# A two-layer decoder trunk: a new beginning, the exponential's table loaded ahead of the attention, and the compression's inner chain in five VectorE operations

## Chip, cores and metric

The kernel runs on 1 core of one Trainium2 chip. The time is the device time of one execution in microseconds (us); less is better.

## What is computed

A trunk of two layers over 256 tokens of width 1024, in float32. Each layer norms x, multiplies it by one wide matrix, and cuts the result into the inputs of two attentions and two merge gates:

```python
def hybrid_layer(x, ...):
    h = rms_norm(x, attn_pre_gain)
    u = h @ w_in
    (qa, ka, va, qb, kcb, vcb, ksb, vsb, kwb, vwb, g_nsa, g_a, g_b) = jnp.split(u, offsets, axis=-1)
    o_a = swa_sink_attention(rope(qa), rope(ka), va, attn_sinks)
    kc = compress(kcb, cmp_pos_emb[0], cmp_w1[0], cmp_b1[0], cmp_w2[0])
    vc = compress(vcb, cmp_pos_emb[1], cmp_w1[1], cmp_b1[1], cmp_w2[1])
    o_b = nsa_attention(qb, rope(qb), kc, vc, rope(ksb), vsb, rope(kwb), vwb, sigmoid(g_nsa))
    mixed = jax.nn.sigmoid(g_a) * (o_a @ w_branch_a) + jax.nn.sigmoid(g_b) * (o_b @ w_branch_b)
    x = x + rms_norm(mixed @ w_out, attn_post_gain)
    x = x + rms_norm(conv_ffn(rms_norm(x, ffn_pre_gain), ...), ffn_post_gain)

def compress(t, pos_emb, w1, b1, w2):
    # blocks of 32 tokens at a stride of 16, flattened
    hid = jax.nn.gelu((blocks + pos_emb) @ w1 + b1, approximate=True)
    return hid @ w2
```

The calls that are cut or shortened here (`...`, `rope`) are as their names say. The compression turns the 256 tokens into 15 blocks for keys and again for values, in each layer: four chains of it in all.

## The kernel before, in words

**Products in three parts.** Every float32 operand is split into a rounded high part and the remainder, the low part, and each product is three TensorE matmuls: high by high (L366), high by low weight (L367), low x by high weight (L368). The 256 tokens are two row blocks of 128, called t = 0 and 1.

**Weights.** The stream `W` holds all weights in the order of use. A chunk is loaded (`load`) by a DMA issued on SyncE's queue (SP) into one of four buffers `st`; ScalarE copies it to the rounded `wh` (L114, through `copy`), VectorE subtracts to get `wl` (L117, through `sub`). These two lines are helpers: the same lines stand for every such split in the kernel. `make` does both, `high` does ScalarE's part and hands back VectorE's.

**Input projection.** `w_in` is cut into nine tiles of up to 512 columns (`IN_TILES`); a tile has four chunks c of two 128-row steps, and for each chunk the two row blocks t, so 4 x 2 x 2 x 3 = 48 matmuls. What follows a tile is its `fin_...`: for the first, queries of the first attention, a rotation (`rope`, L466 to L470), the split of the result (`q_rot`) and, some ticks later, transposes on TensorE (L477) whose result ScalarE copies to SBUF. The third tile to be computed holds the columns from 1536 on.

**Order.** A clock counts the parts of work that the program writes out; `later(n, fn)` puts `fn` n ticks behind. For most of the program the framework's scheduler then orders instructions by its own rules; in the first tile the written order is kept on TensorE, VectorE and ScalarE (`MANUAL0`). The first tile takes its parts (t, c) in the order `FIRST`, and `HOOKS` says what comes ahead of which part: the steps 1, 2, 3 (make that weight chunk), B, C, D (transpose and split another quarter of X) and r (`rest`: norms of the rows, the rope tables).

**Beginning** (`start`, from L1117). TensorE runs 6 matmuls of zeros (`warm`, L1124), a transpose of the gain, four transposes of X's first quarter (`first_T`, L410; one quarter is 128 rows by 512 columns), then 8 more matmuls of zeros, and then the first tile. X comes in three transfers: the first quarter on ScalarE's queue, the second on SP behind W0, the other half of X on SP behind W1. Then W2, W3 and the small inputs follow on SP. `table(fn)` (L270, L271) runs a one-element activation so that ScalarE loads that function's table: Sin at the start, for the rope tables.

**First attention.** `Unit.scores` runs score matmuls (L595), a row minimum on VectorE for each head (L604) and an exponential on ScalarE (L607). The first exponential makes ScalarE load that table, since the sine's is in place.

**Compression** (`cmp_hidden_T`, from L724). Two transposes, a VectorE copy out of PSUM (L733), then nine operations of GpSimd (POOL, L736 to L747): three add up a bias, three add shifted parts of the hidden values to it, and three build the cubic in the tanh of the gelu. Some ticks later `cmp_gelu` runs the tanh on ScalarE (L753) and VectorE goes on from there (L754).

## Time and profile before

| | us |
|---|---|
| three runs | 791.46, 794.11, 797.75 |
| their median | 794.11 |
| the profiled execution, its own time | 794.85 |
| its span in the profile | 793.0 |

The span is the time from the first to the last instruction in the trace; the execution's own time is 1.85 us longer, for what lies around it. In the profile the engines are PE (TensorE), PEld (its weight load), DVE (VectorE), ACT (ScalarE), POOL (GpSimd) and SP (SyncE). PEclk is the clock granted to TensorE as a share of full speed. A wait is shown as [idle before <-what ended it]. A row such as "x3" at its end is a group of three instructions of the same kind, and its duration is theirs together.

### The profile page before, as it was taken

The numbers are of one execution on the slowest core, as the hardware profiler recorded it, in microseconds if no ns is written. First come the engines' busy times: TensorE is split into PE (matmuls) and PEld (weight loads), VectorE is DVE, ScalarE is ACT, GpSimd is POOL, SyncE is SP. The second block draws the span as 40 slices with busy tenths as digits, with TensorE's granted clock in tenths as the row PEclk, the third lists the DMA queues.
The fourth block names the chain that finished last, engine by engine and source line by source line (L and its number), as shares of the span: only waits on it lengthen the run. The fifth ranks groups of instructions, "written<-read, shape, count | busy, mean of one in ns | idle before, by whom it ended". The sixth has DMA issues, their size and how long they took to land.

```text
span 793.0 us, 12908 instructions
## 1 busy us (share of the span) xinstructions
PE 765.7 (97%) x4745; PEld 682.0 (86%) x4745; DVE 613.2 (77%) x1168; ACT 495.4 (62%) x948; POOL 48.1 (6%) x96
## 2 busy tenths in 40 slices
PE   8999999999899999999989999999998999999996
PEld 6689888888699999999868889888877999999995
DVE  5898888676778767777788888886867877778775
ACT  4678877744666555665555879767555655556552
POOL 2300022100100000000010000230001000000000
PEclk9999999999999999999999999999999999999999
DMA  7633156456556656666435232644645666656731
GB/s 268 218 111 123 41 160 216 144 172 205 166 168 196 187 185 183 209 218 186 157 118 173 74 121 86 206 151 135 205 137 182 193 185 186 186 184 212 216 105 53
DMA packets 42202, 131.26 MB, mean 166 GB/s; under 512 B 5359, under 2 KB 5915, under 8 KB 42139
## 3 DMA queue, kind: packets, MB, share of 16 engines
q1 hardware_dynamic: 41995, 130.18, 51.4%
q8 instruction: 37, 0.61, 0.3%
q10 hardware_dynamic: 144, 0.26, 0.1%
q14 instruction: 26, 0.21, 0.1%
HBM read 129.37 MB, written 1.05 MB: 164 GB/s over the span
## 4 chain that ended last, share of the span: by engine, by line
PE 81%; DVE 7%; ACT 7%; POOL 2%; issue 2%; DMA 1%; SPq 0%; DVEq 0%; POOLq 0%; ACTq 0%
PE mm L366 6%; PE mm L367 6%; PE mm L368 6%; PE S L367 5%; PE S L368 5%; PE S L366 5%; PE T L1000 5%; PE T L999 5%; PE mm L1000 5%; PE mm L999 5%; PE T L998 5%; PE mm L998 5%; PE O L366 3%; PE O L367 3%; PE O L368 3%; DVE wl L117 2%
## 5 line engine op out<-in xcount | busy, mean ns | idle before, releaser
L117 DVE TENSOR_TENSOR wl<-st,wh 128x1024 fp32r<-128x1024 f32 (+2 forms) x226 | 268.0, 1188 | 101.1 <-ACT wh L114 99.7
L114 ACT ACTIVATE wh<-st 128x1024 fp32r<-128x1024 f32 (+2 forms) x226 | 231.8, 1029 | 170.9 <-PE O L368 40.1
L366 PE MATMUL mm<-wh,x 128*128 128x512 f32 (+2 forms) x256 | 97.3, 382 | 0.1
L367 PE MATMUL mm<-wl,x 128*128 128x512 f32 (+2 forms) x256 | 96.2, 376 | 0.0
L368 PE MATMUL mm<-wh,x 128*128 128x512 f32 (+2 forms) x256 | 95.2, 372 | 0.0
L999 PE MATMUL mm<-q,wh 128*128 128x256 f32 x320 | 90.7, 283 | 0.0
L999 PE MATMUL T<-q,wh 128*128 128x256 f32 x320 | 90.6, 283 | 0.0
L1000 PE MATMUL T<-q,wl 128*128 128x256 f32 x320 | 90.6, 283 | 0.0
L1000 PE MATMUL mm<-q,wl 128*128 128x256 f32 x320 | 90.5, 283 | 0.0
L998 PE MATMUL T<-q,wh 128*128 128x256 f32 x320 | 90.5, 283 | 0.0
L998 PE MATMUL mm<-q,wh 128*128 128x256 f32 x320 | 90.4, 283 | 0.0
L998 PEld LDWEIGHTS mm<-q,wh 128*128 128x128 f32 x320 | 61.3, 192 | 0.9
L998 PEld LDWEIGHTS T<-q,wh 128*128 128x128 f32 x320 | 61.4, 192 | 0.8
L999 PEld LDWEIGHTS mm<-q,wh 128*128 128x128 f32 x320 | 61.3, 192 | 0.8
L999 PEld LDWEIGHTS T<-q,wh 128*128 128x128 f32 x320 | 61.4, 192 | 0.7
L1000 PEld LDWEIGHTS mm<-q,wl 128*128 128x128 f32 x320 | 61.3, 192 | 0.1
L1000 PEld LDWEIGHTS T<-q,wl 128*128 128x128 f32 x320 | 61.4, 192 | 0.0
L368 PEld LDWEIGHTS mm<-wh,x 128*128 128x128 f32 x256 | 49.2, 192 | 6.3
L366 PEld LDWEIGHTS mm<-wh,x 128*128 128x128 f32 x256 | 49.2, 193 | 5.8 <-ACT k L114 0.4
L367 PEld LDWEIGHTS mm<-wl,x 128*128 128x128 f32 x256 | 49.4, 193 | 5.6 <-DVE wl L117 0.3
L607 ACT ACTIVATE k<-k,mn 128x128 f32<-128x128 f32 (+1 forms) x96 | 42.5, 446 | 8.4 <-DVE mn L604 8.4
L354 POOL TENSOR_SCALAR rstd<-s 128x1 f32<-128x1 f32 x16 | 6.1, 381 | 520.7 <-ACT k L362 520.5
(293 smaller groups left out, 1672.9 us busy)
## 6 DMA issues: line engine op xcount, KB each, us to landing
st<-in_ffn_w_up_dram SPq DMA_DIRECT2D x88, 512.0 KB, 4.3
st<-in_w_in_dram SPq DMA_DIRECT2D x48, 512.0 KB, 3.8
st<-in_ffn_w_down_dram SPq DMA_DIRECT2D x44, 512.0 KB, 4.3
st<-in_w_out_dram SPq DMA_DIRECT2D x16, 512.0 KB, 3.6
st<-in_w_in_dram SPq DMA_DIRECT2D x16, 384.0 KB, 3.1
st<-in_cmp_w_dram SPq DMA_DIRECT2D x16, 256.0 KB, 2.6
st<-in_w_branch_a_dram SPq DMA_DIRECT2D x8, 512.0 KB, 3.6
st<-in_w_branch_b_dram SPq DMA_DIRECT2D x8, 512.0 KB, 3.6
```

The costliest lines, as they stand in the source:

```text
L114: act.activation(dst, src, AF.Copy, scale=scale)
L117: dve.tensor_tensor(dst, a, b, ALU.subtract)
L354: pool.tensor_scalar(r, s2[:, 0:1], s2[:, 1:2], EPS, ALU.add, ALU.add)
L366: pe.matmul(o, xh, wh, start=first, stop=False, skip_group_check=True)
L367: pe.matmul(o, xh, wl, start=False, stop=False, skip_group_check=True)
L368: pe.matmul(o, xl, wh, start=False, stop=last, skip_group_check=True)
L607: last_exp[0] = act.activation(self.pt[:, hh, s, :], sm[:, :nk], AF.Exp, bias=self.mn[:, i:i + 1], scale=-1.0, accum_out=self.dn[:, i:i + 1])
L998: pe.matmul(o, wh[:, k, :], hh[:, k, c0:c1], start=(k == 0), stop=False, skip_group_check=True)
L999: pe.matmul(o, wh[:, k, :], hl[:, k, c0:c1], start=False, stop=False, skip_group_check=True)
L1000: pe.matmul(o, wl[:, k, :], hh[:, k, c0:c1], start=False, stop=(k == 7), skip_group_check=True)
```

## The change

It has three parts. **First, the beginning.** All four quarters of X are issued on ScalarE's queue, the two first halves ahead of the two second halves, and W0 to W3 alone stand first on SP. Chunks 4 to 9 are loaded early, right behind the small constants, into buffers that later hold other things (tags "sg" and "kB"), not into the four `st`. `WARM` becomes 6, 2 and 3 matmuls, with X's transposes between them. The first two chunks of the first tile are no longer done part by part but by `products`: for chunk 0, both row blocks are taken in the order high by high, high by low weight, low x by high weight; for chunk 1 each row block has high by high, low x by high weight, high by low weight. The second halves of X are transposed in one step (`second`) ahead of the third part, W3 is made ahead of the fifth, and `rest` ahead of the sixth.

**Second, the table of the exponential.** `table(AF.Exp)` is run behind the rope tables in layer 1, and behind the first copy of the first tile's rotation for t = 1 in layer 2. **Third, the compression.** The nine POOL operations become five on VectorE, each with two arithmetic steps; the bias b1 is added in the third of them.

```diff
...
-WARM = (6, 8)
-HOOKS = {0: '1C', 1: 'B2', 2: 'D', 6: '3r'}
-FIRST = [(0, 0), (0, 1), (1, 0), (1, 1), (0, 2), (1, 2), (0, 3), (1, 3)]
+WARM = (6, 2, 3)
+FIRST = [(0, 0), (1, 0), (0, 1), (1, 1), (0, 2), (1, 2), (0, 3), (1, 3)]
+EARLY = {4: ("sg", 2), 6: ("sg", 2), 8: ("kB", 1)}
 CMPI = (0, 0, 0, 0, 4, 6, 7, 8)
...
     def copy(dst, src, scale=1.0):
-        act.activation(dst, src, AF.Copy, scale=scale)
+        return act.activation(dst, src, AF.Copy, scale=scale)
...
     class Stream:
         def __init__(self):
             self.specs, self.loaded, self.made, self.used, self.front = [], {}, {}, 0, 0
+            self.room = {}
         def add(self, src, a, b, tag="w", ahead=2):
             self.specs.append((src, a, b, tag, ahead))
...
         def load(self, i):
             src, a, b, tag, _ = self.specs[i]
-            st = wp.tile([P, a, b], F32, tag="st", bufs=4, name=nm("st"))
+            st = self.room.pop(i, None)
+            if st is None:
+                st = wp.tile([P, a, b], F32, tag="st", bufs=4, name=nm("st"))
             nc.sync.dma_start(st, src)
             self.loaded[i] = st, a, b, tag
+        def early(self, i, tag, bufs):
+            both = ap_.tile([P, 2, 2, 512], F32, tag=tag, bufs=bufs, name=nm("early"))
+            self.room[i], self.room[i + 1] = both[:, 0], both[:, 1]
         def make(self, i=None):
             i = self.front if i is None else i
...
     pool.memset(rows, 0.0)
     grow = k1()[0:KD, 0:P]
     nc.sync.dma_start(cst[:, 0:P], consts[:, 0:P])
-    act.dma_start(halves(X[:, 0, :])[0], halves(xv[:, 0, :])[0])
     nc.sync.dma_start(grow, attn_pre_gain[0].rearrange("(k p) -> k p", p=P))
-    W.load(0)
-    nc.sync.dma_start(halves(X[:, 0, :])[1], halves(xv[:, 0, :])[1])
-    W.load(1)
-    nc.sync.dma_start(X[:, 1, :], xv[:, 1, :])
-    W.load(2)
-    W.load(3)
+    for h in range(2):
+        for t in range(2):
+            act.dma_start(halves(X[:, t, :])[h], halves(xv[:, t, :])[h])
+    for i in range(4):
+        W.load(i)
     last_sq = [None]
     def table(fn):
...
     nc.sync.dma_start(cst[:, P:], consts[:, P:])
     sink = cp.tile([P, DEPTH, 8], F32, name="sink")
     nc.sync.dma_start(sink, attn_sinks.partition_broadcast(P))
+    for i, (tag, bufs) in EARLY.items():
+        W.early(i, tag, bufs)
+        W.load(i)
+        W.load(i + 1)
     row_load(R_B1, cmp_b1.rearrange("l k h -> (l k) h"))
     row_load(R_POS, cmp_pos_emb.rearrange("l k (pr two) d -> (l k pr) (two d)", two=2))
...
         SG = [ap_.tile([P, QKV], F32, tag="sg", bufs=2, name=nm("SG")) for _ in range(2)]
         done = set()
+        def products(t, c, bk, chs, w):
+            todo = [(tt, p, k) for p in ((0, 0), (0, 1), (1, 0)) for tt in range(2) for k in range(2)] if c == 0 else \
+                   [(t, p, k) for p in ((0, 0), (1, 0), (0, 1)) for k in range(2)]
+            if c == 0:
+                todo = todo[6 * t:6 * t + 6]
+            for tt, (xp_, wp_), k in todo:
+                tk = slice(tt * P, (tt + 1) * P)
+                pe.matmul(bk[tt][:, :w], (xh, xl)[xp_][:, 2 * c + k, tk], chs[c][wp_][:, k, :],
+                          start=(c == k == xp_ == wp_ == 0), stop=False, skip_group_check=True)
         def in_tile(i, tag, fin, tmajor=False, hooks={}):
             c0, w = IN_TILES[i]
             bk = [bank(tag) for _ in range(2)]
...
                     chs[c] = W.next(2, w)
                 ch = chs[c]
                 tk = slice(t * P, (t + 1) * P)
+                if first and i == 0 and c < 2:
+                    products(t, c, bk, chs, w)
+                    return
                 for k in range(2):
                     kk = 2 * c + k
                     o, wh, wl = bk[t][:, :w], ch[0][:, k, :], ch[1][:, k, :]
...
                 done.add(key)
             return fn
-        def q_rot(qT, t, h0, src, key, delays):
+        def q_rot(qT, t, h0, src, key, delays, exp_after=None):
             d = rope(src, t, True, 4 * len(delays))
             for i, delay in enumerate(delays):
                 stk = k2(F32R)
                 sv = stk.rearrange("p (h a d) -> p h a d", h=4, a=2)
                 di = d[:, 4 * i:4 * i + 4, :]
-                copy(sv[:, :, 0, :], di)
+                hi = copy(sv[:, :, 0, :], di)
+                if exp_after is not None:
+                    with tc.issue_after(hi.ins):
+                        table(exp_after)
+                    exp_after = None
                 sub(sv[:, :, 1, :], di, r32(sv[:, :, 0, :]))
                 h = h0 + 4 * i
                 later(delay, stack_T(stk, qT[:, h:h + 4, t * P:(t + 1) * P], (key[0], t, h // 4), 0))
...
         def fin_a(t, b):
-            q_rot(qA, t, 0, heads(b, 0, 8), ("qA", t, 0), (DL["qa0"], DL["qa1"]))
+            q_rot(qA, t, 0, heads(b, 0, 8), ("qA", t, 0), (DL["qa0"], DL["qa1"]), AF.Exp if t == 1 and not first else None)
         def fin_b(t, b):
             k_rot(t, heads(b, 0, 2), [(kA, ("kA", t), DL["ka"])])
...
             dve.tensor_copy(hs, tb[:, 0:160])
             bs = small("bs", 1, 2)
             b1 = vec[:, R_B1 + l * 2 + kd:R_B1 + l * 2 + kd + 1]
-            pool.tensor_tensor(bs, hs[:, 2:3], hs[:, 12:13], ALU.add)
-            pool.tensor_tensor(bs, bs, hs[:, 82:83], ALU.add)
-            pool.tensor_tensor(bs, bs, b1, ALU.add)
+            dve.scalar_tensor_tensor(bs, hs[:, 2:3], hs[:, 12:13], hs[:, 82:83], ALU.add, ALU.add)
             z, z3 = small("z", 32, 2), small("z3", 32, 2)
             hg = hs.rearrange("p (s c k) -> p s k c", s=2, k=5)
             zg = z.rearrange("p (g c) -> p g c", g=2)
-            pool.tensor_scalar(zg, hg[:, 0, 3:5, :], bs, None, ALU.add)
-            pool.tensor_tensor(zg, zg, hg[:, 0, 0:2, :], ALU.add)
-            pool.tensor_tensor(zg, zg, hg[:, 1, 0:2, :], ALU.add)
-            pool.tensor_tensor(z3, z, z, ALU.mult)
-            pool.tensor_scalar(z3, z3, 0.044715, 1.0, ALU.mult, ALU.add)
-            pool.tensor_tensor(z3, z3, z, ALU.mult)
+            dve.scalar_tensor_tensor(zg, hg[:, 0, 3:5, :], bs, hg[:, 0, 0:2, :], ALU.add, ALU.add)
+            dve.scalar_tensor_tensor(zg, hg[:, 1, 0:2, :], b1, zg, ALU.add, ALU.add)
+            dve.scalar_tensor_tensor(z3, z, 0.044715, z, ALU.mult, ALU.mult)
+            dve.scalar_tensor_tensor(z3, z3, 1.0, z, ALU.add, ALU.mult)
             cc["z", kd] = (z, z3)
             later(DL["ge"], lambda: cmp_gelu(kd))
...
         gb = bank("T")
         pe.transpose(gb[:, 0:KD], grow, ident[0:KD, 0:KD])
         dve.tensor_copy(gfirst, gb[:, 0:KD])
-        low = first_split(0, 0, first_T(0, 0), xp)
+        m0 = first_T(0, 0)
+        lw0 = W.high(0)
+        low0 = first_split(0, 0, m0, xp)
         warm(WARM[1])
-        lw = W.high(0)
-        low()
-        lw()
-        def xs(*args):
-            lows = [first_split(t, h, first_T(t, h), xp) for t, h in args]
+        low1 = first_split(1, 0, first_T(1, 0), xp)
+        warm(WARM[2])
+        lw0()
+        low0()
+        low1()
+        W.make(1)
+        def second():
+            m0, m1 = first_T(0, 1), first_T(1, 1)
+            lw = W.high(2)
+            lows = [first_split(t, 1, m, xp) for t, m in ((0, m0), (1, m1))]
+            lw()
             for f in lows:
                 f()
...
                 rs[t] = rstd_of(mean_sq(halves(X[:, t, :])))
             dve.tensor_scalar(nsink, sink, -1.0, None, ALU.mult)
             rope_tables()
-        act_ = {"B": lambda: xs((0, 1)), "C": lambda: xs((1, 0)), "D": lambda: xs((1, 1)), "X": lambda: xs((1, 0), (1, 1)),
-                "1": lambda: W.make(1), "2": lambda: W.make(2), "3": lambda: W.make(3), "r": rest, "w": lambda: warm(3)}
-        return {FIRST[i]: [act_[c] for c in h] for i, h in HOOKS.items()}
+            table(AF.Exp)
+        steps = {2: [second], 4: [lambda: W.make(3)], 5: [rest]}
+        return {FIRST[i]: fns for i, fns in steps.items()}
     more_rows()
     later(20, lambda: load_vec(0, 4))
```

On TensorE, at the program's start (S: products of zeros; T: transposes; mm: the first tile of t = 0 and 1; wh, wl: W0's parts; x_8 or x_11: X's high part; x_9 or x_12: its low part), before:

```order
L1124 MATMUL S_128<-k_61_126 128x512 x6
L1128 MATMUL T_135<-cst,k_2_76 128x8
L410 MATMUL T_138<-cst,X 128x128 x4
L1124 MATMUL S_128<-k_61_126 128x512 x8
L410 MATMUL T_165<-cst,X 128x128 x4
L366 MATMUL mm_159<-wh_154,x_8_108 128x512
L367 MATMUL mm_159<-wl_155,x_8_108 128x512
L368 MATMUL mm_159<-wh_154,x_9_109 128x512
L410 MATMUL T_180<-cst,X 128x128 x4
```

and after:

```order
L1148 MATMUL S_138<-k_64_136 128x512 x6
L1152 MATMUL T_145<-cst,k_2_76 128x8
L420 MATMUL T_148<-cst,X 128x128 x4
L1148 MATMUL S_138<-k_64_136 128x512 x2
L420 MATMUL T_161<-cst,X 128x128 x4
L1148 MATMUL S_138<-k_64_136 128x512 x3
L445 MATMUL mm_179<-wh_155,x_11_118 128x512 x2
L445 MATMUL mm_180<-wh_155,x_11_118 128x512 x2
L445 MATMUL mm_179<-wl_156,x_11_118 128x512 x2
L445 MATMUL mm_180<-wl_156,x_11_118 128x512 x2
L445 MATMUL mm_179<-wh_155,x_12_119 128x512 x2
```

Eight zero products stood between the first transposes and the first tile; two and three stand there now, with X's other transposes between them, and the products run by operand parts, over both row blocks.

On ScalarE, at the first attention of layer 1 (L607 before and L635 after are the exponentials; q_15 to q_19 are the transposed queries), before:

```order
L114 ACTIVATE k_174_584<-k_170_575 128x2x128
L607 ACT_TABLE_LOAD
L607 ACTIVATE k_176_589,dn_591<-k_180_601,mn_590 128x128
L607 ACTIVATE k_176_589,dn_591<-k_181_604,mn_590 128x128
L607 ACTIVATE k_176_589,dn_591<-k_182_607,mn_590 128x128
L607 ACTIVATE k_176_589,dn_591<-k_183_610,mn_590 128x128
L612 ACTIVATE co_613<-co_613 128x4
L114 ACTIVATE q_15_118<-T_616 128x4x128
L114 ACTIVATE q_16_119<-T_622 128x4x128
```

and after:

```order
L114 ACTIVATE q_18_128<-T_613 128x4x128
L114 ACTIVATE VT_114<-mm_456,rstd_241 128x4x64
L114 ACTIVATE k_170_578<-k_168_572 128x2x128
L114 ACTIVATE k_172_581<-k_168_572 128x2x128
L635 ACTIVATE k_174_586,dn_588<-k_178_598,mn_587 128x128
L635 ACTIVATE k_174_586,dn_588<-k_179_601,mn_587 128x128
L114 ACTIVATE q_19_129<-T_619 128x4x128
L635 ACTIVATE k_174_586,dn_588<-k_180_604,mn_587 128x128
L635 ACTIVATE k_174_586,dn_588<-k_181_607,mn_587 128x128
L640 ACTIVATE co_610<-co_610 128x4
```

The table load in front of the exponentials is gone, and the copies of q, which stood behind four exponentials, stand ahead of the first and between the second and the third. The load is now found further up on ScalarE, between the sine (L353, L354) and the rounding of weights:

```order
L353 ACTIVATE k_92_254<-k_92_254 128x64
L114 ACTIVATE wh_358<-early_101 128x1024
L354 ACTIVATE k_92_254<-k_92_254 128x64
L277 ACT_TABLE_LOAD
L277 ACTIVATE warm_275<-neg_half 128x1
L114 ACTIVATE wh_374<-early_104 128x1024
```

In the compression, POOL before (the sixth of the nine, of the same form as the fifth, is not shown):

```order
L736 TENSOR_TENSOR bs_1396<-hs_1394 128x1
L737 TENSOR_TENSOR bs_1396<-bs_1396,hs_1394 128x1
L738 TENSOR_TENSOR bs_1396<-bs_1396,vec 128x1
L742 TENSOR_SCALAR z_1400<-hs_1394,bs_1396 128x32
L743 TENSOR_TENSOR z_1400<-z_1400,hs_1394 128x32
L745 TENSOR_TENSOR z_385_1401<-z_1400 128x32
L746 TENSOR_SCALAR z_385_1401<-z_385_1401 128x32
L747 TENSOR_TENSOR z_385_1401<-z_385_1401,z_1400 128x32
```

and VectorE after, from the copy out of PSUM on (co: the end of a softmax; wj, wl: low weights):

```order
L761 COPY hs_1391<-T_1388 128x160
L764 SCALAR_TENSOR_TENSOR bs_1393<-hs_1391 128x1
L648 TENSOR_SCALAR co_1443<-dn_1365 128x4
L117 TENSOR_TENSOR M_5401<-vec,M_5401 128x8x2
L768 SCALAR_TENSOR_TENSOR z_1395<-hs_1391,bs_1393 128x32
L649 TENSOR_TENSOR co_1443<-co_1443,ge_870 128x4
L769 SCALAR_TENSOR_TENSOR z_1395<-hs_1391,vec,z_1395 128x32
L654 RECIPROCAL co_1443<-co_1443 128x4
L770 SCALAR_TENSOR_TENSOR z_383_1396<-z_1395 128x32
L117 TENSOR_TENSOR wl_1434<-st_1431,wh_1433 128x768
L771 SCALAR_TENSOR_TENSOR z_383_1396<-z_383_1396,z_1395 128x32
```

The nine rows of POOL are gone, and five of VectorE stand between rows that were there before.

## Rows read from the trace of the kernel before

**Rows 1.** The page's busy times: engine, busy us, share of the span, instructions.
```profile
PE 765.7 (97%) x4745; PEld 682.0 (86%) x4745; DVE 613.2 (77%) x1168; ACT 495.4 (62%) x948; POOL 48.1 (6%) x96
```

**Rows 2.** TensorE's waits, whole span: line, what was waited for, us, times, longest.
```profile
PE S L718 <- DVE mn L604: 3.3, 2, 1.7
...
PE T L477 <- ACT q L114: 2.4, 2, 1.3
PE S L367 <- DVE wl L117: 1.9, 2, 1.4
...
PE T L410 <- DMA X<-in_x_dram: 1.4, 1, 1.4
```

**Rows 3.** Timeline of TensorE to 40 us: start, duration, instruction, idle before.
```profile
5.83 3.58 PE L1124 MATMUL S<-k 128*128 128x512 f32 x8
...
11.16 0.48 PE L366 MATMUL mm<-wh,x 128*128 128x512 f32 x1
...
16.07 0.39 PE L368 MATMUL mm<-wh,x 128*128 128x512 f32 x1
...
18.11 0.39 PE L368 MATMUL mm<-wh,x 128*128 128x512 f32 x1
...
28.88 0.50 PE L367 MATMUL S<-wl,x 128*128 128x512 f32 x1 [1.44 <-DVE wl L117]
...
37.52 0.40 PE L366 MATMUL mm<-wh,x 128*128 128x512 f32 x1
```

**Rows 4.** Windows: stretch, us, busy PE PEld DVE ACT POOL, PEclk, DMA share, GB/s.
```profile
55.00:60.00 5.00, 3.92 (x23) 3.68 (x22) 4.47 (x24) 5.00 (x21) 0.00 (x0) 0.69 0.00 0
445.00:450.00 5.00, 4.83 (x28) 4.80 (x29) 4.50 (x23) 5.00 (x21) 0.00 (x0) 0.66 0.00 0
```

**Rows 5.** Timeline of ScalarE and VectorE in the first 30 us.
```profile
6.93 0.63 ACT L114 ACTIVATE x<-k 128x512 fp32r<-128x512 f32 x1 [4.27 <-DVE k L412]
7.47 1.04 ACT L114 ACTIVATE wh<-st 128x1024 fp32r<-128x1024 f32 x1
...
8.54 1.23 DVE L117 TENSOR_TENSOR wl<-st,wh 128x1024 fp32r<-128x1024 f32 x1 [0.25 <-ACT wh L114]
...
26.15 0.75 DVE L466 SCALAR_TENSOR_TENSOR k<-mm,rstd,tab 128x512 f32<-128x512 f32 x1 [1.82 <-POOL tab L348]
```

**Rows 6.** DMA view of the first 30 us, in 40 slices of 0.75 us.
```profile
GB/s 0 0 42 229 396 393 194 115 292 377 388 399 426 432 410 359 271 153 51 61 262 360 355 366 317 366 71 0 5 295 378 65 0 55 306 321 200 169 276 153
```

**Rows 7.** Timeline of ScalarE, then TensorE, at layer 1's first attention.
```profile
52.77 1.28 ACT L607 ACT_TABLE_LOAD   x1
54.06 0.40 ACT L607 ACTIVATE k<-k,mn 128x128 f32<-128x128 f32 x1
...
54.72 0.29 PE L366 MATMUL mm<-wh,x 128*128 128x280 f32 x1
54.84 0.29 PE L367 MATMUL mm<-wl,x 128*128 128x280 f32 x1
...
56.34 0.53 PE L477 MATMUL T<-ident_r,k 128*128 128x128 f32 x4 [1.08 <-ACT q L114]
...
59.42 0.43 PE L368 MATMUL mm<-wh,x 128*128 128x280 f32 x1
59.65 0.43 PE L366 MATMUL mm<-wh,x 128*128 128x280 f32 x1
```

**Rows 8.** Timeline of the first compression chain of layer 1, 108 to 117 us.
```profile
108.46 0.56 POOL L736 TENSOR_TENSOR bs<-hs 128x1 f32<-128x1 f32 x1 [2.57 <-DVE hs L733]
...
110.15 1.07 POOL L743 TENSOR_TENSOR z<-z,hs 128x32 f32<-128x32 f32 x1
...
113.16 0.23 ACT L753 ACTIVATE z<-z 128x32 f32<-128x32 f32 x1 [3.21 <-POOL z L747]
113.42 0.19 DVE L754 SCALAR_TENSOR_TENSOR z<-z,z 128x32 f32<-128x32 f32 x1 [1.38 <-ACT z L753]
...
116.17 0.67 PE L718 MATMUL S<-wj,M 128*80 128x256 f32 x4 [1.68 <-DVE mn L604]
```

## The prediction

> **What bounds the kernel now.** I read the page's busy times first, then TensorE's waits, then the timeline at each long wait. TensorE is busy 97% of the span [rows 1], so only three things can shorten the run: fewer TensorE instructions, less idle time on TensorE, or more time at its higher clock. The change leaves the arithmetic of TensorE as it is. What remains to be won is small: in the waits [rows 2] the four that the change touches hold 3.3 us (compression, twice), 2.4 us (transposes of the first attention, twice), 1.9 us (split weights of the second tile) and 1.4 us (X, before the first product). To that come two things no list of waits shows. The first real product starts only at 11.16 us [rows 3], after 14 warm-up matmuls. And in two stretches of 5 us the granted clock is 0.69 and 0.66 [rows 4], so some 3.1 and 3.4 us of them run at 1.2 instead of 2.4 GHz (5 x 0.31 / 0.5 and 5 x 0.34 / 0.5); each lies at the wait in the first attention of its layer. The long rest of the products the change does not touch.
>
> **The beginning.** It ends, for this sum, where the third tile's first product stands: 37.52 us [rows 3]. A product of 512 columns takes 0.227 us at full clock (9 of them from 16.07 to 18.11 us [rows 3]). Until then TensorE has 96 of them, 21.8 us, and four groups of four transposes, some 0.3 us a group (an estimate: its 4 x 128 columns are those of one product, and the copy behind it costs a little more).
> When does the first product start after the change? It needs the rounded W0 and the rounded X of rows 0, half 0. ScalarE now rounds W0 first. W0 had landed by 7.47 us when ScalarE took it [rows 5]; now three more quarters of X (256 KB each) travel on ScalarE's queue beside it, and at the 390 GB/s of that moment [rows 6] one quarter is 0.65 us. Bounds: 7.5 us if none goes ahead of W0, 9.4 us if all three do; I take one, the quarter that is issued next to it, so 8.1. Then 1.04 us for W0 and 0.63 us for X [rows 5]: first product at 9.8 us, 1.4 us earlier than now.
> The first 12 products come in the order hi, lo weights, lo X. Their last operand, the low part of X for the other 128 rows, needs W0's low part (1.23 us [rows 5]) and two low parts of X (half the columns, 0.6 us or so each) on VectorE behind W0's rounding, so they end near 12.6 us. Then eight transposes in one go, with the copies that their products need first (0.6 and 0.6 us), 36 products of the first tile (8.2 us) and 48 of the second (10.9 us): 32.9 us, and one group of transposes, 33.2 us. The present stalls inside this stretch go: VectorE reached the rope of the first tile at 26.15 us, after waiting for POOL's table, and held the low weights of the second tile behind it, so TensorE waited 1.44 us [rows 3, 5]. In the new order all four low parts of the second tile stand ahead of the rope, and their loads (the "early" ones) are issued right behind the first four. 37.5 - 33.2 = 4.3 us. One group of transposes that was done before 37.52 us now comes later: 4.0 us.
> Against it: the warm-up matmuls go from 14 to 11, and pauses open between them, because the second transposes wait for a quarter of X. The eight at 5.83 us took 0.45 us each [rows 3], the lower clock; the higher one was there at 11.16 us. If it is not there at 9.8 us, up to 12 products cost 0.2 us more each, 2.4 us; of that a part hides behind their own operands. I take 0.7 us. **Term: 3.3 us**, with bounds of 5 us (W0 as early as now) and -1 us (W0 last, and the clock late). VectorE must keep the lead too: when it comes to its rope it has done three more low weights than now, 3.7 us of work that is no longer behind the rope.
>
> **The table of the exponential.** The load of 1.28 us stands between the last rotation copy and the first exponential, 52.77 to 54.06 us, and behind both ScalarE's copies of q are late; TensorE waits 1.08 us for them at 56.34 us [rows 7], and 2.4 - 1.1 = 1.3 us in the second layer [rows 2]. Products of 280 columns, which followed each other every 0.12 us before the stall (54.72 to 54.84 us), then do so every 0.23 us (59.42 to 59.65 us [rows 7]): half clock, for the 3.1 and 3.4 us from above, of which half is lost, 3.2 us in all. So 2.4 + 3.2 = 5.6 us hang on the two stalls. Taking the load away moves ScalarE 1.28 us ahead, more than the first stall and as much as the second; in the new order the first copy of q also stands ahead of all exponentials and the second between them, where both stood behind four. The load now stands behind the sine in layer 1, and in layer 2 behind a copy of the first tile's rotation; at both places ScalarE (62% busy over the span [rows 1]) rounds weights ahead of their use, so I cost it at nothing there; were that cover gone, it would be 1.3 us each. What is late next is ScalarE itself and VectorE: in those stretches they are busy 5.00 and 4.5 of the 5 us [rows 4], so TensorE cannot use all of the gift. I take 70%: **4.0 us**, bounds 0 and 5.6.
> The Trainium skill's page "ScalarE: Activation LUTs", section "What ACT_TABLE_LOAD costs", adds a drain of about 1.38 us to each load. Here the exponential starts 0.01 us after the load [rows 7], so the trace does not show it; by the page the load would cost 2.7 us at its new places, and the sum would be worse by at most the 1.4 us that the cover there might not hold.
>
> **The compression's chain.** Nine POOL operations run from 108.46 us to ScalarE's tanh at 113.16 us, one of them 1.07 us long; ScalarE stood idle 3.21 us before the tanh, VectorE 1.38 us before the operation behind it, and TensorE 1.68 us at 116.17 us [rows 8]. In layer 2 the wait is 3.3 - 1.7 = 1.6 us [rows 2]. Now five VectorE operations, 0.19 us each by the same kind of operation at 113.42 us [rows 8], are placed between others: 0.95 us more on VectorE per chain, four chains. In the first chain of a layer VectorE had that time, it was idle for 1.4 us; the tanh comes about 2 us earlier, the scores' minimum for which TensorE waited some 1.3 us earlier. In the second chain nobody waited; VectorE there pays 0.95 us that TensorE's products cover. Twice 1.3, less 0.2: **2.4 us**, bounds 3.3 (the whole wait) and -1.9 (two chains' own time, uncovered).
>
> **Sum.** 3.3 + 4.0 + 2.4 = 9.7 us. The profiled execution took 794.85 us, span and what lies around it, 0.7 us above the median of the three runs (794.11); 794.85 - 9.7 = 785.15, I say 785.0 us.
>
> **Rivals.**
> First: the beginning gives nothing. For it: X and W0 share the same 390 GB/s [rows 6], all of X is now issued at once, and W1 moves behind as much of X; with fewer warm-up matmuls the first products run slow. Against it: the 1.44 us stall of the second tile goes in any case. Time: 785.0 + 3.3 = 788.3 us. Chance 0.16.
> Second: the slow clock does not go with these stalls. For it: the waits of 1.4 us at 28.88 us and of 1.68 us at 116.17 us [rows 3, 8] are longer than the one of 1.08 us, and no slow stretch follows them; so what else TensorE did counts, and another pause may bring the slow stretch in place of these. Time: 785.0 + 3.2 = 788.2 us. Chance 0.12. The Trainium skill's "TensorE: Matmul & The Clock Gate", section "What's actually happening", says that the monitor runs free of the kernel's start, which is this rival.
> Third, slower: VectorE becomes the bound in the compression. The order there puts one or two low weights (1.23 us each) and the five small operations ahead of the multiplication that ends a softmax, and TensorE's transposes wait for that: up to 1.23 + 0.95 = 2.2 us in each of four chains, 8.8 us, with a slow-clock stretch behind each (1.6 us each, as above), 15 us in all. It decides once the chains cost more than the 7.3 us of the two other terms, that is 1.8 us per chain: 785.0 + 2.4 + 15 = 802 us. Against it: VectorE is busy 77% of the span [rows 1] and was idle at the first chain. Chance 0.07.
>
> **How the numbers follow.** The forecast has 0.65, with its own range of 781 to 788 us. A measurement of this kernel tells about 1% from no change, that is 786.2 us on the median. Nine tenths of the forecast's chance lies below that, 0.59, and 0.03 of the first two rivals': faster 0.62. The third rival is slower, 0.07; the rest, 0.31, is within 1%. The range for 8 in 10 takes in both middle rivals and the better bounds of the beginning and the table: 779.5 to 790.5 us.
>
> **What would show it.** In the new profile: the first product near 9.8 us and the third tile's near 33.2 us; no wait above 0.3 us between them; no table load before the first exponential, no wait of q's transposes, and a granted clock of 1.0 in both attention stretches; the tanh at most 3 us after the copy out of PSUM that begins the chain, and the compression's TensorE wait under 0.5 us. I am wrong if the third tile starts after 36 us, if a slow stretch stays, or if new TensorE waits for VectorE appear in the attention or the compression.

## The result, and the profile after

The changed kernel takes 784.01 us, the median of four runs (782.47 to 785.31), where before takes 794.39 in the same comparison: a ratio of 0.9869, with a 95% interval of 0.984 to 0.9898. In a second comparison on another occasion (experiment r_after below) it was 784.15 us and 0.9881, 0.986 to 0.9901. By the two ratios the change brings 10.4 and 9.4 us. The forecast was 785.0 us. The sum was right to a microsecond; two of its three terms were too small and one was more than twice too large.

The profiled execution of the changed kernel took 782.81 us with a span of 781.0. Its busy times, from the page:

```profile
PE 759.2 (97%) x4742; PEld 676.8 (87%) x4742; DVE 613.1 (79%) x1188; ACT 495.4 (63%) x950; POOL 34.0 (4%) x60
```

Against [rows 1], POOL has lost 14.1 us and VectorE is as busy as before although it has 20 instructions more; TensorE has lost 6.5 us of busy time with the same products; less of it runs at 1.2 GHz (mean granted clock 0.998, 0.992 before) and three warm-up products are gone. TensorE's waits over the whole span (line, what was waited for, us in total, times, longest):

```profile
PE T L383 <- DVE k L415: 2.9, 2, 1.6
...
PE T L501 <- DVE k L117: 1.1, 2, 1.0
...
PE T L501 <- ACT k L114: 0.7, 1, 0.7
PE mm L445 <- ACT x L114: 0.7, 1, 0.7
PE mm L376 <- DVE VT L546: 0.6, 1, 0.6
PE T L501 <- ACT q L114: 0.6, 1, 0.6
```

Of the four waits of [rows 2] three are gone and the one for a copy of q is down from 2.4 to 0.6 us. Beside it stand four new ones of 0.6 to 1.0 us: one in front of the first product, one in the second tile, and two in the attention (VT, the values, in layer 1; k in layer 2). L383 is a wait at the change of layers that before has too.

TensorE in the first 33 us (start, duration, instruction, idle before), to be read against [rows 3]:

```profile
6.63 0.94 PE L1148 MATMUL S<-k 128*128 128x512 f32 x3
8.23 1.26 PE L445 MATMUL mm<-wh,x 128*128 128x512 f32 x4 [0.66 <-ACT x L114]
9.32 1.09 PE L445 MATMUL mm<-wl,x 128*128 128x512 f32 x4
10.25 1.08 PE L445 MATMUL mm<-wh,x 128*128 128x512 f32 x4
11.17 1.03 PE L420 MATMUL T<-cst,X 128*128 128x128 f32 x8
...
29.77 0.51 PE L501 MATMUL T<-ident_r,k 128*128 128x128 f32 x4 [0.98 <-DVE k L117]
...
32.70 0.39 PE L376 MATMUL mm<-wh,x 128*128 128x512 f32 x1
```

The first product starts at 8.23 us (11.16 before), the twelve of the first chunk follow each other every 0.245 us on the mean ((11.17 - 8.23) / 12), which is nearly full speed, and the third tile begins at 32.70 us, 4.8 us earlier. Between the two no product waits, but the transposes of the first rotation do, 0.98 us at 29.77 us, where the forecast had no wait above 0.3 us. ScalarE and VectorE there, against [rows 5]:

```profile
6.60 1.06 ACT L114 ACTIVATE wh<-st 128x1024 fp32r<-128x1024 f32 x1 [2.49 <-DMA st<-in_w_in_dram]
...
7.56 1.13 ACT L114 ACTIVATE x<-k 128x512 fp32r<-128x512 f32 x2
...
22.09 1.21 DVE L117 TENSOR_TENSOR wl<-early,wh 128x1024 fp32r<-128x1024 f32 x1
24.89 0.75 DVE L490 SCALAR_TENSOR_TENSOR k<-mm,rstd,tab 128x512 f32<-128x512 f32 x1 [1.59 <-POOL tab L358]
```

W0 is there at 6.60 us. VectorE still waits for POOL's table of the rope (1.59 us, 1.82 before). The low weights of the second tile's first chunks are done by then, so no product waits for them; what is late now are the rope's own transposes, the 0.98 us above: VectorE makes two more low weights (26.34 and 28.08 us, 1.22 us each) among the steps of the rotation, ahead of its low part, at 29.21 us, for which they wait. The two stretches around the first attention (columns as in [rows 4]), and the two waits in layer 2:

```profile
50.00:55.00 5.00, 4.36 (x36) 4.16 (x36) 4.51 (x22) 5.00 (x22) 0.00 (x0) 1.00 0.00 0
435.00:440.00 5.00, 4.28 (x35) 4.06 (x34) 4.75 (x24) 4.90 (x20) 0.00 (x0) 1.00 0.01 3
```

```profile
433.45 0.54 PE L501 MATMUL T<-ident_r,k 128*128 128x128 f32 x4 [0.62 <-ACT q L114]
436.89 0.28 PE L501 MATMUL T<-ident_r,k 128*128 128x128 f32 x1 [0.72 <-ACT k L114]
```

The granted clock is 1.0 in both stretches, 0.69 and 0.66 before. But ScalarE is nearly as full as before (5.00 and 4.90 of 5 us), and the waits of layer 2, 0.62 + 0.72, add up to the 1.34 us that stood there in one piece. The first compression chain of layer 1, against [rows 8]:

```profile
101.96 0.32 DVE L761 COPY hs<-T 128x160 f32<-128x160 f32 x1
...
102.79 0.21 DVE L764 SCALAR_TENSOR_TENSOR bs<-hs 128x1 f32<-128x1 f32 x1
...
104.92 0.18 DVE L771 SCALAR_TENSOR_TENSOR z<-z,z 128x32 f32<-128x32 f32 x1
105.14 0.23 ACT L777 ACTIVATE z<-z 128x32 f32<-128x32 f32 x1 [0.76 <-DVE z L771]
...
107.99 0.63 PE L746 MATMUL S<-wj,M 128*80 128x256 f32 x4
```

The tanh starts 3.2 us after the copy that begins the chain. ScalarE was idle 0.76 us ahead of it (3.21 before), and TensorE's L746 waits for nothing.

**Where the time went.** The products in three parts (L366 to L368 before; L376 to L378 and L445 after) are 1878 in every trace, and their order differs only among near neighbours, never at the places below; so the same product can be looked for in each timeline. The table gives how much earlier than in the profile of before it starts, in us, at the third tile's first product (the 97th), behind the crowded part of layer 1's attention (261st), behind layer 1's compression (385th), and at three such places in layer 2 (1041st, 1241st, 1351st; the 1041st lies behind the change of layers). The columns from e_begin on are the experiments below.

| product | before starts | after | e_begin | e_table | e_comp | r_after | r_notable | e_nocomp |
|---|---|---|---|---|---|---|---|---|
| 97 | 37.52 | 4.82 | 4.86 | 0.22 | -1.21 | 4.79 | 4.75 | 5.19 |
| 261 | 91.57 | 6.12 | 5.63 | 1.78 | 0.09 | 6.06 | 5.55 | 6.50 |
| 385 | 140.53 | 7.81 | 5.29 | 1.71 | 1.79 | 7.73 | 7.23 | 6.43 |
| 1041 | 428.61 | 9.05 | 6.54 | 2.88 | 1.70 | 7.82 | 8.45 | 5.23 |
| 1241 | 498.56 | 10.30 | 7.87 | 4.16 | 1.74 | 9.10 | 8.53 | 6.52 |
| 1351 | 538.42 | 12.11 | 7.65 | 2.44 | 3.55 | 10.89 | 10.33 | 5.19 |

From 385 to 1041, where of the whole change only the table's load in layer 2 falls, the profile of after gains another 1.2 us, and so does e_begin, which has the load late: before has a slow-clock stretch at the change of layers (granted clock 0.66 from 400 to 405 us), after has none there. Kernel r_after is the same code with that stretch in it again: it gains 0.1 us there, and seven of the fourteen profiles have such a stretch at that place. That piece is luck of the execution and no part of the change, and so is e_comp's loss of 1.2 us ahead of the 97th product (granted clock 0.66 from 10 to 15 us, behind a wait for X).

### The profile page after: what moved, and what is told of

Same layout as the page of the kernel before. It is cut to its first block, busy times and chain, and to the rows that moved or that the text cites. A ratio compares the mean times of both kernels' runs of the same rounds, so it can differ in the third digit from the quotient of the medians.

```text
span 781.0 us, 12886 instructions
## 1 busy us (share of the span) xinstructions
PE 759.2 (97%) x4742; PEld 676.8 (87%) x4742; DVE 613.1 (79%) x1188; ACT 495.4 (63%) x950; POOL 34.0 (4%) x60
## 4 chain that ended last, share of the span: by engine, by line
PE 83%; ACT 8%; DVE 4%; POOL 2%; issue 1%; DMA 1%; SPq 0%; DVEq 0%; POOLq 0%; ACTq 0%
PE mm L376 6%; PE mm L378 6%; PE mm L377 6%; PE T L1024 5%; PE mm L1023 5%; PE T L1023 5%; PE mm L1024 5%; PE T L1022 5%; PE mm L1022 5%; PE S L377 5%; PE S L376 5%; PE S L378 5%; PE O L376 3%; PE O L377 3%; PE O L378 3%; ACT k L635 2%
## 5 line engine op out<-in xcount | busy, mean ns | idle before, releaser
L117 DVE TENSOR_TENSOR wl<-st,wh 128x1024 fp32r<-128x1024 f32 (+2 forms) x220 | 260.4, 1186 | 101.5 <-ACT wh L114 100.3
L114 ACT ACTIVATE wh<-st 128x1024 fp32r<-128x1024 f32 (+2 forms) x220 | 225.5, 1028 | 178.1 <-PE O L378 40.5
L376 PE MATMUL mm<-wh,x 128*128 128x512 f32 (+2 forms) x248 | 92.9, 375 | 0.7 <-DVE VT L546 0.6
L377 PE MATMUL mm<-wl,x 128*128 128x512 f32 (+2 forms) x248 | 91.6, 370 | 0.0
L378 PE MATMUL mm<-wh,x 128*128 128x512 f32 (+2 forms) x248 | 91.3, 368 | 0.1
L378 PEld LDWEIGHTS mm<-wh,x 128*128 128x128 f32 x248 | 46.7, 188 | 6.1 <-DVE x L117 0.5
L376 PEld LDWEIGHTS mm<-wh,x 128*128 128x128 f32 x248 | 46.7, 188 | 6.0 <-issue 0.8
L377 PEld LDWEIGHTS mm<-wl,x 128*128 128x128 f32 x248 | 46.7, 188 | 4.8
L635 ACT ACTIVATE k<-k,mn 128x128 f32<-128x128 f32 (+1 forms) x96 | 42.4, 445 | 7.1 <-DVE mn L632 7.0
L114 ACT ACTIVATE k<-k 128x256 fp32r<-128x256 f32 x72 | 29.1, 413 | 9.1 <-DVE k L1035 5.6
```

Source lines behind the costliest of these rows:

```text
L114: return act.activation(dst, src, AF.Copy, scale=scale)
L117: dve.tensor_tensor(dst, a, b, ALU.subtract)
L376: pe.matmul(o, xh, wh, start=first, stop=False, skip_group_check=True)
L377: pe.matmul(o, xh, wl, start=False, stop=False, skip_group_check=True)
L378: pe.matmul(o, xl, wh, start=False, stop=last, skip_group_check=True)
L635: last_exp[0] = act.activation(self.pt[:, hh, s, :], sm[:, :nk], AF.Exp, bias=self.mn[:, i:i + 1], scale=-1.0, accum_out=self.dn[:, i:i + 1])
```

## The experiments

Four theories were weighed: that the three parts add up as the prediction has them; that the table's part does not deliver, since other waits stand behind it; that the slow clock does not hang on those waits; and that in the beginning the early loads, the order or the warm-up carry the gain.

**One part alone: e_begin, e_table, e_comp.** Each is the kernel before with one part of the change.

```diff
 # e_begin: the change without these
-            table(AF.Exp)                   # layer 1
-            q_rot(..., AF.Exp if t == 1 and not first else None)
+            q_rot(...)                      # layer 2
-            dve.scalar_tensor_tensor(...)   # five, as the nine pool operations of before
 # e_table: before, with these alone
+            table(AF.Exp)                   # layer 1
+                    with tc.issue_after(hi.ins):
+                        table(exp_after)    # layer 2
 # e_comp: before, with the five VectorE operations alone
```

> The kernel before with only the new beginning (transfers of X, early loads, order of the first products, warm-up of 6, 2 and 3). Theory, three terms that add: the third tile's first product at 32.7 us as in the full change (37.52 before), of which some 0.8 us is given back before the attention; the load of the exponential's table still stands before the first exponential and TensorE still waits about 1 us for a copy of q in each layer, with a half-clock stretch behind it; the compression's waits of 1.7 and 1.6 us stay. Time 4 to 5 us under before, 789.5 to 790.5. Rival, the new order of the beginning is what also moved the copies of q ahead and so did the attention's work: attention waits under 0.3 us here already, 786.5 to 788.

> The kernel before with only the exponential's table loaded ahead (layer 1 behind the rope tables, layer 2 behind the first rotation's copy). Theory: the two waits for the copies of q (1.08 and 1.34 us) fall to about 0.6 us each, the half-clock stretches behind them go; gain 1.3 to 1.7 us in the attention of layer 1 and 1.25 us in that of layer 2, 2.5 to 3 us in all, so 791.4 to 791.9. Rival, the slow stretches do not hang on these waits: the granted clock stays below 0.8 in the stretch behind at least one of them, and the gain is under 1.3 us (793.1 or more). Second rival, the full 4.0 us of the prediction: 790.4.

> The kernel before with only the compression's chain as five VectorE operations. Theory: the wait of TensorE for the scores' minimum (1.68 us in layer 1, 1.6 in layer 2) goes whole, as the page of the full change has no such wait; 1.7 + 1.8 = 3.5 us, so 790.9. Rival of the prediction, VectorE pays for its five operations: 2.4 us or less, 792.0 or more. Tanh within 3 us of the copy out of PSUM that begins the chain.

Measured: e_begin 788.15 us, ratio 0.9926 (0.9907 to 0.9945), that is 5.9 us of 794.3; e_table 793.47 us, 0.9991 (0.9978 to 1.0005), 0.7 us; e_comp 790.56 us, 0.9953 (0.9935 to 0.9971), 3.7 us. The sum, 10.3 us, is what the whole change brings: the parts add, within intervals of 1 to 1.5 us each. The compression came as its theory had it (790.9 us). The beginning lies between its theory (789.5 to 790.5 us) and its rival (786.5 to 788); at the 385th product, ahead of the pieces of luck, it is 5.3 us. The table gives hardly anything. In e_begin's timeline (waits over the span):

```profile
PE S L746 <- DVE mn L632: 3.3, 2, 1.7
...
PE T L501 <- ACT q L114: 1.3, 1, 1.3
```

Of the two waits for a copy of q one is left, that of layer 2: in layer 1 the beginning alone has taken it away. In e_table's list:

```profile
PE S L599 <- ACT k L114: 1.5, 1, 1.5
...
PE T L477 <- ACT k L114: 1.4, 2, 0.7
PE T L477 <- ACT q L114: 1.1, 2, 0.6
```

The two waits for q, 2.4 us before, are now four, two for q and two for k, 1.1 + 1.4 = 2.5 us: by itself the early table buys no waiting time in either layer. No slow stretch stands behind them, as the theory had it; the gain of under 1.3 us is the rival's. The wait of L599, which before doesn't have, is in the compression of layer 2 (512.32 us), where e_table loses 1.7 us from the 1241st to the 1351st product and so gives back what it won. In e_comp both waits for the scores' minimum are gone, and the wait for q in layer 1 stands as before, this time with a granted clock of 1.00 in the 10 us behind it:

```profile
57.57 0.54 PE L477 MATMUL T<-ident_r,k 128*128 128x128 f32 x4 [1.09 <-ACT q L114]
```

```profile
55.00:60.00 5.00, 3.77 (x30) 3.39 (x30) 4.45 (x24) 4.99 (x19) 0.00 (x0) 1.00 0.00 0
```

From the 97th to the 261st product e_comp gains 1.30 us on before, with the wait in place. So that is what the slow stretch costs there, and e_begin, which has neither the wait nor the stretch, gains only 0.77 us: the new beginning gives back 0.5 us on the way.

**The engine or the number of operations: e_dve9.** The changed kernel with the nine old operations on VectorE.

```diff
-            dve.scalar_tensor_tensor(bs, ...)
+            dve.tensor_tensor(bs, hs[:, 2:3], hs[:, 12:13], ALU.add)
...
+            dve.tensor_tensor(z3, z3, z, ALU.mult)
```

> The changed kernel with the nine old operations of the compression's chain, but on VectorE. Theory, the engine counts and not the number of operations (no handing over to POOL and back, no long POOL operation): four more small operations of 0.1 to 0.2 us on VectorE in each chain cost 0.4 to 0.8 us of chain, covered; time within 0.7 us of the changed kernel, 784.0 to 784.7. Rival, the count is what makes the gain: half of the 3.5 us comes back, 785.5 to 786.

Measured 786.32 us, ratio 0.9895 (0.9876 to 0.9915): by the time neither theory. The timeline tells more. Its beginning is that of the changed kernel, but the first product came late, at 9.06 us, behind late transposes of X, and the first four stand some 0.4 us apart, near half speed:

```profile
9.06 1.82 PE L445 MATMUL mm<-wh,x 128*128 128x512 f32 x4
...
10.72 1.08 PE L445 MATMUL mm<-wl,x 128*128 128x512 f32 x4
```

That cost 1.4 us at the third tile, 0.8 us by the late first product and the rest by the slow four, and has nothing to do with the chain. From the 261st to the 385th product e_dve9 gains 1.7 us on before, as after does; from the 1241st to the 1351st 1.4 us, after 1.8. So the engine makes most of it and the number some 0.4 us, from two profiles only.

**The table part taken out of the change: e_notable, r_notable, with r_after beside it, and e_table1.**

```diff
 # e_notable, r_notable
-            table(AF.Exp)
-            q_rot(..., AF.Exp if t == 1 and not first else None)
+            q_rot(...)
 # e_table1: only the second of the two, so layer 1 keeps its early table
 # r_after: the changed kernel, no edit
```

> The changed kernel without its table part: the exponential's table is loaded in front of the first exponential again. Theory, formed from the profiles of the kernels with one part each: the load only hid behind other waits, since in the layers' attention the part leaves waits of 0.62 and 0.72 us where it takes one of 1.3 away, and the slow-clock stretches do not hang on that wait; time within 1 us of the changed kernel, 783.5 to 785.2, and in its profile the single wait of about 1.3 us for a copy of q in layer 2 is back, while the attention of both layers takes as long to within 0.4 us. Rival, the prediction's 4.0 us: 788.0.

> The changed kernel again, beside the next kernel on one chip, to weigh the table part by itself. If the part is worth under 1 us, the two ratios differ by less than 0.0015 and the granted clocks of both kernels' executions lie in the same band; if it is worth the prediction's 4.0 us, by 0.005, with a lower clock in the kernel without it.

> The changed kernel without its table part, again. Theory: ratio within 0.0015 of the changed kernel's in the same call. Rival one, the wait of 1.3 us in layer 2 brings a slow-clock stretch in most executions: mean granted clock lower by 0.002 (1.7 us) than the changed kernel's, ratio higher by 0.002. Rival two, the prediction's 4.0 us: ratio higher by 0.005.

> The changed kernel with the table moved in layer 1 only; in layer 2 the load stands before the first exponential again. Theory: what the table part is worth (1.7 us between the two kernels of the last call) comes from layer 2 alone, where the wait of 1.3 us for a copy of q is back and with it, in most executions, a slow-clock stretch; ratio as without the part, 0.9895 to 0.9905, and in the profile a granted clock below 0.95 in the 10 us behind that wait. Rival, layer 1 carries it: ratio as the changed kernel's, 0.987 to 0.9885, and no wait of over 0.7 us for q in layer 2.

Measured: e_notable 784.88 us, 0.9899 (0.988 to 0.9919); r_after 784.15 us, 0.9881 (0.986 to 0.9901); r_notable 785.81 us, 0.9899 (0.9883 to 0.9916); e_table1 785.53 us, 0.9895 (0.9879 to 0.9912). Between r_after and r_notable, measured side by side, lie 1.7 us; the intervals overlap, but the three kernels without the table in layer 2 agree (0.9895 to 0.9899) and the two runs of the changed one lie below them (0.9869, 0.9881). The profile says where. In r_notable, layer 2:

```profile
436.72 0.54 PE L501 MATMUL T<-ident_r,k 128*128 128x128 f32 x4 [1.34 <-ACT q L114]
```

```profile
435.00:440.00 5.00, 3.66 (x22) 3.44 (x21) 4.47 (x22) 5.00 (x21) 0.00 (x0) 0.72 0.00 0
440.00:445.00 5.00, 5.00 (x39) 5.00 (x39) 4.56 (x14) 4.36 (x16) 0.00 (x0) 0.93 0.01 3
```

The mean granted clock of the four executions is 0.994, r_after's 0.996. From the 1041st to the 1241st product r_notable takes 69.87 us, r_after 68.67: the slow stretch costs 1.2 us. And in e_begin, with the same wait at 438.64 us:

```profile
435.00:440.00 5.00, 3.63 (x28) 3.17 (x27) 4.46 (x24) 4.97 (x16) 0.00 (x0) 1.00 0.03 11
440.00:445.00 5.00, 5.00 (x43) 5.00 (x42) 4.56 (x20) 5.00 (x22) 0.00 (x0) 1.00 0.01 3
```

There the clock stayed up, and from the 1041st to the 1241st product e_begin gains 1.33 us on before, after 1.25 and r_after 1.28, all of it clock that before lost there. So the early table buys no waiting time in layer 2. What it buys there goes with the split of the pause into 0.62 and 0.72 us: of the six kernels profiled with the wait of 1.34 us in one piece (before, e_begin, e_comp, e_notable, r_notable, e_table1) all but e_begin show a slow stretch right behind it; of the eight others none. The first rival of r_notable's expectation, then, and for layer 2 the theory of e_table1; e_notable's theory had the time right (784.88 us) and the clock wrong. The other 0.5 us are layer 1's, against e_table1's theory: from the 97th to the 261st product the kernels with the new beginning and the early table take 52.75 to 52.81 us (after, r_after, e_nocomp, e_dve9, e_table1, e_warm0 below), those without the table 53.26 to 53.33 (e_begin, e_notable, r_notable), all at a granted clock of 1.00. No wait in TensorE's list shows where, and e_table1's time, in another comparison than r_notable's, is too coarse to tell.

**The beginning taken apart: e_noearly, e_warm0.** The changed kernel without the early loads, and without the warm-up.

```diff
 # e_noearly
-EARLY = {4: ("sg", 2), 6: ("sg", 2), 8: ("kB", 1)}
+EARLY = {}
 # e_warm0
-WARM = (6, 2, 3)
+WARM = (0, 0, 0)
```

> The changed kernel without the early loads: chunks 4 to 9 go through the four weight buffers behind the small rows, and on VectorE the second to fourth low weights of the second tile stand behind the first rotation again. Theory, the early loads are what lets the second tile run without a stop: first product unchanged near 8.2 us, a wait of 1 to 2 us for a low weight in the second tile, third tile's first product at 34.2 to 34.7 us (32.70 with them), time 785.7 to 786.5. Rival, the order of the first tile alone does it: third tile at 33 us or less, time as the changed kernel's.

> The changed kernel without the eleven warm-up products. Theory of the prediction (the clock is low at the first products unless TensorE was kept busy): the granted clock stands below 1.0 in some stretch of the first 15 us and the first twelve products take near 0.45 us each; third tile's first product 1.5 to 3 us later than 32.70 us, time 785.5 to 787. Rival, the warm-up is of no use: the first product at 8.2 us and the third tile within 0.5 us of 32.70.

e_noearly: 785.69 us, 0.9911 (0.9891 to 0.9931). Its first product is at 8.08 us, and in the second tile one wait is back:

```profile
24.43 0.50 PE L377 MATMUL S<-wl,x 128*128 128x512 f32 x1 [1.20 <-DVE wl L117]
...
33.56 0.39 PE L376 MATMUL mm<-wh,x 128*128 128x512 f32 x1
```

The third tile comes at 33.56 us instead of 32.70: 0.9 us for the early loads there, and 1.2 us by the 261st product (4.87 us ahead of before, where after is 6.12 ahead). The early loads did not take the whole wait of a product away: 1.20 us for a low weight became 0.98 us for a transpose, so most of that wait only changed its place. A part of the 0.9 us is order: e_noearly does two groups of the rotation's transposes ahead of the third tile (26.59 and 31.80 us), the changed kernel one. In layer 1's attention e_noearly waits 0.81 us for q and 0.64 us for k, the changed kernel 0.65 us for VT. The theory's mechanism, at a smaller size. e_warm0: 784.09 us, 0.989 (0.9873 to 0.9907). Its first products:

```profile
8.00 2.07 PE L445 MATMUL mm<-wh,x 128*128 128x512 f32 x4 [1.59 <-ACT x L114]
9.87 1.76 PE L445 MATMUL mm<-wl,x 128*128 128x512 f32 x4
11.47 1.10 PE L445 MATMUL mm<-wh,x 128*128 128x512 f32 x4
```

Eight of the first twelve products follow each other every 0.47 and 0.40 us; with the warm-up all do every 0.245 on the mean. The third tile starts at 33.97 us, 1.3 us late, and that is still there behind the attention. So the prediction's mechanism holds and the warm-up of eleven products is worth about 1.3 us in the profile; the median of four runs (784.05 to 784.29) does not show it, with a mean granted clock of 0.998 in each of them, where the changed kernel's eight runs have 0.995 to 0.998. Compared at one clock it does: the two of the eight at 0.998 took 782.81 and 782.40 us, 1.2 to 1.9 us less. Why all four runs here kept the clock later on is not shown.

**What is late next: e_kpool.** The changed kernel with the rotated keys' rounding copies on POOL.

```diff
-                copy(sv[:, :, 0], kb)
+                pool.tensor_copy(sv[:, :, 0], kb)
```

> The changed kernel with the rounding copies of the rotated keys on POOL in place of ScalarE (the same numbers). It asks what is late next in the attention. Theory, ScalarE is (busy 5.0 of 5 us in two of these stretches): its 3 copies per row block, 0.4 us each, go, the waits of 0.6 to 0.7 us for ScalarE shrink, and the attention of a layer is 0.5 to 1 us shorter, time 782 to 783.5. Rival, POOL is slower in such a copy and shares its reads with VectorE: the copy takes over 0.8 us, new waits of TensorE for the keys, time 784.5 to 787.

Measured 784.53 us, 0.9899 (0.9878 to 0.992): not better. From its waits:

```profile
PE T L501 <- POOL k L537: 2.5, 4, 1.0
```

A copy takes 0.40 us on POOL, as on ScalarE, so the rival's price is wrong; but TensorE now waits for POOL four times. In layer 2 the copy starts 0.16 us behind the end of the rotation on VectorE (437.51 and 437.67 us); on ScalarE, in the changed kernel, 0.57 us behind it (435.86 and 436.43 us). So ScalarE did hold that copy by some 0.4 us, but with the edit the rotation itself comes about 1 us later against the products, and the run does not tell what the copy alone is worth.

**The compression taken out: e_nocomp.** The changed kernel with the nine POOL operations, the same edit as in e_comp the other way.

> The changed kernel with the compression's chain of nine POOL operations again. Theory, the three parts add: the waits of 1.7 and 1.6 us for the scores' minimum are back, 3.5 us by the two kernels' timelines, ratio higher than the changed kernel's by 0.0044. Rival, in the faster kernel the chain has more room: under 2 us, 0.0025.

Measured 788.88 us, 0.9935 (0.9914 to 0.9955), 0.0054 or 4.3 us above r_after beside it; the theory had 0.0044. Both waits for the scores' minimum are back, and with them the one that e_table showed:

```profile
PE S L746 <- DVE mn L632: 3.3, 2, 1.7
...
PE S L623 <- ACT k L114: 1.2, 1, 1.2
```

So the early table and the POOL chain disturb each other in layer 2's compression, by waits of 1.2 to 1.5 us. Neither has it alone: e_begin, with the POOL chain and the late table, and after, with the early table and no such chain, lack that wait. Which order of the instructions makes it was not tested.

## Why the prediction was right, point by point

- **The bound.** Right. TensorE is still 97% busy, and what was won is waits and clock.
- **The beginning, 3.3 us: right in kind, too small.** It measured 4.8 us at the third tile and 5.9 us (4.4 to 7.4) alone, 5.3 us of it at the 385th product. Four steps of the sum were off. "The quarter that is issued next to it" was to go ahead of W0; W0 was rounded from 6.60 us on, not from 8.1, so the first product came at 8.23 and not at 9.8. The 7.47 us of before was ScalarE's own time: it took X first, and W0's transfer had ended at 5.86 us by the trace; I read it as the time of landing. The 0.7 us for a late clock were not lost in nine of the ten profiles with this warm-up, where at most one of the first twelve products stands 0.4 us or more ahead of the next; e_dve9 is the tenth, so that term was a risk and no constant. The 1.44 us stall went as foretold, but 0.98 us came back as a wait of the rotation's transposes. And the gain does not end at the third tile: e_begin has neither the wait for q nor the slow stretch in layer 1's attention, which the sum had put under the table; by the 261st product it is 5.6 us.
- **The table, 4.0 us: the step that failed.** It measured 0.7 us alone (-0.4 to 1.7) and 1.7 us inside the change. The step was "5.6 us hang on the two stalls", with 70% of it (3.9 us) to be had. The 2.4 us of waiting among them gave nothing: layer 1's wait went with the beginning already, in layer 2 the wait only broke in two, 0.62 + 0.72 for 1.34 us, and e_table has 2.5 us for 2.4. The next copies are late by themselves. "What is late next is ScalarE itself and VectorE" was said, but as a discount of 30% and not as all of it. ScalarE in layer 2 of after:

```profile
431.81 0.73 ACT L114 ACTIVATE k<-k 128x256 fp32r<-128x256 f32 x2
432.44 0.39 ACT L635 ACTIVATE k<-k,mn 128x128 f32<-128x128 f32 x1
...
432.82 1.07 ACT L114 ACTIVATE q<-T 128x512 fp32r<-128x512 f32 x2
...
435.87 0.66 ACT L114 ACTIVATE wh<-st 128x560 fp32r<-128x560 f32 x1
436.43 0.71 ACT L114 ACTIVATE k<-k 128x256 fp32r<-128x256 f32 x2
```

  The transposes of q ended at 431.60 us; their copies come 1.2 us later, behind two copies of k and the first exponential. The order that the sum counted on, a copy of q ahead of all exponentials, is layer 1's alone. The copy of k at 436.43 us stands behind the rounding of a weight. Of the 3.2 us of clock, layer 2's holds, 1.2 to 1.3 us in five executions of six; layer 1's 1.3 us do not need this part, since e_comp has that wait (1.09 us) and no slow stretch. The 0.5 us that the early table does win in layer 1 hang on neither.
- **The compression, 2.4 us: right in kind, too small.** It measured 3.7 us (2.3 to 5.2) alone and 4.3 us inside the change. The whole wait goes, 1.7 and 1.6 us (3.5 us from the 261st to the 385th and from the 1241st to the 1351st product of e_comp). The 0.95 us per chain that VectorE pays is covered in all four chains, and where I took 1.3 of each wait nothing else stood in its way. The added part inside the change is the wait of 1.2 us for ScalarE that the old chain brings beside the early table.
- **The rivals.** The beginning gave something. The third, VectorE as the bound of the compression, did not come: TensorE's waits for VectorE there (M) are as long as before, 0.5 and 0.2 us at most. The second, that the slow clock does not go with these stalls, is half true: the stretch at the change of layers comes and goes in the same code (after and r_after), and the wait of 1.34 us has it in r_notable and not in e_begin. The Trainium skill's page "TensorE: Matmul & The Clock Gate", section "What's actually happening", says that the gate's monitor runs free of the kernel's start, so that the point of a change varies between executions. The trace is in line with it, 0.72 and 1.00 behind the same wait in r_notable and e_begin; that this is the cause no run here shows.
- **The table's price at its new places** was taken as nothing. That held. ScalarE in layer 2 of after:

```profile
411.31 1.28 ACT L277 ACT_TABLE_LOAD   x1
412.61 0.20 ACT L277 ACTIVATE warm<-neg_half 128x1 f32<-128x1 f32 x1
```

  The load stands right behind a copy that ends at 411.30 us, ScalarE's next instruction starts 0.02 us behind the load, and TensorE's timeline has no wait from there to 433 us. The drain that the Trainium skill's page "ScalarE: Activation LUTs" (section "What ACT_TABLE_LOAD costs") adds does not show here either.

- **The signs.** Third tile, table load, clock and the compression's wait came as named. The first product came 1.6 us earlier, the tanh 3.2 us behind the copy for at most 3. Three failed: the wait of 0.98 us in the second tile, the wait of 0.62 us for q in layer 2, and a new wait for VectorE in layer 1's attention (VT, 0.65 us), which was to mean "I am wrong". That last one costs nothing that the timelines show: the kernels that have it are those that are 0.5 us faster there.

The total came out by luck: measured one by one, an overestimate of 3.3 us (table) and underestimates of 2.6 (beginning) and 1.3 us (compression) nearly cancel: 9.7 us were forecast, and 10.3 is the sum of the three alone. What stays open: what decides whether the clock falls behind a pause of 1.34 us, since one execution of six went without; where the early table's 0.5 us in layer 1 come from; and how much of a warm-up the beginning needs, since in this order only eleven products and none were tried, and eleven left the clock late in e_dve9.

## What to carry to other kernels

Take a wait off the list only after following what the waiting instruction needs next: if a second producer is ready a microsecond later, the wait splits or moves and the time stays. When an engine takes an operand, ask whether it had landed or the engine had been busy: the two read alike in a timeline and differ in what a new order can win. And test parts one at a time, each alone and each left out: only both together show where two parts disturb each other. Where a slow-clock stretch that comes and goes is worth as much as the part, compare the same stretch of products in several profiles before trusting a median of four.

## What was not expected of the hardware

In e_warm0 the windows report a granted clock of 1.00 from 5 to 10 us, while products of 512 columns stand 0.47 us apart there, twice the 0.227 us of full speed. The first entry for the clock in that trace is the full clock at 11.33 us (5.98 us in after, 10.65 in e_dve9); ahead of it the clock is to be read from the spacing of products. And two pauses of 0.6 to 1.0 us each, 3 to 4 us apart, left the clock at 1.0 in all eight executions profiled with them, where one pause of 1.34 us at the same place did not in five of six. At the change of layers all fourteen have two pauses of up to 1.6 us, some 2 us apart (L383 of after), and seven of them a slow stretch behind. So the length of a pause alone does not tell it.
